# Five split weights and sixteen raw pages instead of seven and twelve in the SwiGLU blocks of a streaming-encoder layer

## The chip, the cores and the metric

The kernel runs on one core of a Trainium2 chip. The metric is the time of one execution on the device in microseconds (us), the median of the timed runs. The engines are TensorE (PE in the profile, PEld its weight loads), VectorE (DVE), ScalarE (ACT), GpSimd (POOL) and SyncE (SP). They run side by side, each through its own list of instructions in order, and wait for one another by semaphores. An instruction that waits holds up all that stands behind it on its engine.

## The reference

One layer on x of 256 rows by 2048 channels, in float32:

```python
x = _layer_norm(ALPHA * x + 0.5 * _swiglu(x, ffn1_w1, ffn1_w3, ffn1_w2), ln1_g, ln1_b)
mix = _hybrid_mixer(x, w_in, b_gates_m, conv_m, norm_m, w_up_m, w_up_sb, w_out)
x = _layer_norm(ALPHA * x + mix, ln2_g, ln2_b)
x = _layer_norm(ALPHA * x + 0.5 * _swiglu(x, ffn2_w1, ffn2_w3, ffn2_w2), ln3_g, ln3_b)
x = x + jax.nn.sigmoid(x @ w_ple_gate) * (p @ w_ple_proj)
```

where `_swiglu(x, w1, w3, w2)` is `(silu(x @ w1) * (x @ w3)) @ w2` with 5632 hidden channels. The mixer joins a chunkwise mLSTM and a stick-breaking attention. Only the two SwiGLU blocks, the first and the third line, have to do with the change.

## The kernel before

**Numbers.** Every float32 operand of a large matmul is split into a high part, rounded to the type that TensorE multiplies fast (fp32r), and a low part, the rest. A product is then three matmuls: high by high, high by low, low by high (L1061 to L1063). Activations stand transposed (`actT`) as the stationary operand, weights stream through.

**Pages.** One pool, `page_pool`, of 44 pages of 128 partitions by 1024 floats holds nearly everything: a raw weight as it was loaded (256 rows by 512 columns, one page), a split weight (two pages, high and low), the activations of 512 channels by 128 rows (one page) and the layer norms' vectors.

**Weights and units.** `program` is one long list. A `Unit` is one weight against 128 rows: two steps in depth of three matmuls, six in all. A plain weight serves two units, one for each half of the 256 rows. The last loop of the kernel (L1043) walks this list and writes each unit's matmuls; behind each unit it writes what has come due on the other engines.

**What a weight passes through.** SyncE loads it (L983, in `loads`). ScalarE writes the high part (L1010) and VectorE the low part (L1014), both in `split_one`. Then TensorE uses it. How far ahead this runs is set by `limits`: `splits_due` places the next split as long as fewer than `SPLIT_FFN` (7 before) split weights are held, counting the one in use. `loads` places the next load as long as fewer than `RAW_FFN` (12 before) raw pages are held and the pages suffice:

```python
while (pos["load"] < most and pos["raw"] < (4 if pos["at"] < 6 else limits(pos["split"])[0])
       and (mixing() or pages[0] + pos["raw"] + 2 * limits(pos["split"])[1] < PAGES - SPARE)):
```

`pages[0]` counts the activations' pages; `SPARE` was 1. In the mixer, and within six weights of the borders between the blocks (`EDGE`), other limits hold. They have names of their own (`RAW_MIX`, `SPLIT_MIX`, `RAW_EDGE`, `SPLIT_EDGE`).

**The SwiGLU blocks.** The hidden channels go in eleven chunks of 512. Three chunks (0, 5, 8) multiply x plainly with w1 and w3. The other eight use a scheme of seven products of half size in place of eight (`seven`, L314, in the manner of Strassen and Winograd), on both halves of the rows, with sums of weights and sums of activations. The sums of weights are made in the raw pages. Some are made by VectorE (L335). Others come by an accumulating transfer that GpSimd issues (L330): the first product's weight is split, then another quarter is added onto its raw page, then it is split again for the fifth product, added to again, split for the sixth, and once more, after a sum at L335, for the fourth. So the four quarter pages of a chunk stay taken from the first product to the fourth. A weight of these products serves one unit. `chained` (L355) strings the products of the eight chunks together, and `weave` (L157) mixes that chain about one to one with the main line: the plain products and those with w2. In the chain the sixth products follow the fifth by seven places.

**What comes due behind a unit.** A chunk's seven products end in three PSUM banks and two that stay (`seeded`). Copies and sums take them apart: L457 and L462 on ScalarE, L451 and L470 on VectorE. The hidden value, the silu of the gate times the up part, is made by VectorE at L473 for the first 128 rows and at L484 for the others. Eight planned microseconds later TensorE transposes it (L266, four matmuls against the identity), ScalarE writes the high part of the transpose (L268) and VectorE the low (L274). From then on the products with w2 may use it; each of them ends in an addition onto the residual (L497). The planner's time (`sched.now`) counts 0.2161 us for each matmul of 512 columns. All these instructions stand in the engines' lists between the splits, at the place where they came due. How many splits stand ahead of them is set by `SPLIT_FFN`.

Of the kernel before, what the change touches and what calls it, by code (L numbers as in the profile page):

```python
# [25 lines left out]
PAGES = 44  # L26
TEMP_BUFS = 6
FORMED = 8
SPARE = 1


RAW_FFN, RAW_MIX, RAW_EDGE = 12, 5, 4
SPLIT_FFN, SPLIT_MIX, SPLIT_EDGE = 7, 6, 11
EDGE = 6
PSUM_BUFS = 6
SKEW = 6
# [144 lines left out]
def kernel(  # L181
# [780 lines left out]
    def mixing():  # L962
        j = pos["split"]
        return any(-EDGE <= j - e < EDGE for e, _ in edges) or [m for e, m in edges if e <= j][-1:] == [True]

    def limits(j):

        if any(-EDGE <= j - e < EDGE for e, _ in edges):
            return RAW_EDGE, SPLIT_EDGE
        mixer = [m for e, m in edges if e <= j][-1:] == [True]  # L970
        return (RAW_MIX, SPLIT_MIX) if mixer else (RAW_FFN, SPLIT_FFN)
# [4 lines left out]
    def loads(most=len(raws)):  # L976
        while (pos["load"] < most and pos["raw"] < (4 if pos["at"] < 6 else limits(pos["split"])[0])
               and (mixing() or pages[0] + pos["raw"] + 2 * limits(pos["split"])[1] < PAGES - SPARE)):
            j = pos["load"]
# [121 lines left out]
```

## Time and profile before

| | us |
|---|---|
| median of 3 timed runs | 2291.09 (2286.04 to 2295.92) |
| profiled execution, its own time | 2298.76 |
| its span, first to last instruction | 2297.0 |
| first SwiGLU block, about | 30 to 700 |
| mixer, about | 700 to 1475 |
| second SwiGLU block, about | 1475 to 2160 |
| busy: TensorE, VectorE, ScalarE, GpSimd | 2228.0, 1681.4, 1231.7, 201.8 |

A row of the profile names the line of the kernel, the engine, the operation, and the tiles it writes and reads (`out<-in`, without buffer numbers), then how many there were. Rows of a timeline begin with start and length in us, and end, in brackets, with how long the engine was idle before and what ended it. Rows of waits name who waited and for whom, the us in total, how many times, and the longest. A stretch gives its ends and its length, then the busy us and the count of instructions for TensorE, its weight loads, VectorE, ScalarE and GpSimd, then the granted clock of TensorE, the busy share of the 16 DMA engines and the GB/s moved.

### The profile page before, as it was taken

Reading aid. Unit: us, or ns where it says so; the run is one execution under the profiler, and the core shown is the slowest. Engines: PE = TensorE matmul, PEld = TensorE weight load, DVE = VectorE, ACT = ScalarE, POOL = GpSimd, SP = SyncE. Lnnn points to the kernel's source line nnn. Section 1 sums busy time; section 2 is a strip of 40 time slices with the busy share of each in tenths; the row PEclk is TensorE's granted clock in tenths of the full one; section 3 lists DMA queues with packets and bytes.
Section 4 is the critical chain, followed back from the end, with each engine's and each line's share of the span. In section 5 each row is a group of like instructions: output and inputs, shape, how many; then the busy total and the mean of one; then the engine's idle time right before and its main releaser. Section 6 shows DMA issues by size and latency. Waiting matters only on the chain. (4 is left out here: it accounts for less than half of the span.)

```text
span 2297.0 us, 27486 instructions
## 1 busy us (share of the span) xinstructions
PE 2228.0 (97%) x10065; PEld 1835.2 (80%) x10065; DVE 1681.4 (73%) x1840; ACT 1231.7 (54%) x1441; POOL 201.8 (9%) x175
## 2 busy tenths in 40 slices
PE   9999989899999999999999999999998989999999
PEld 7878868778887888888888888787886877888878
DVE  6878877788898765654555466787886868889873
ACT  6656545555664555545653354465664555556552
POOL 3111001011100000100100000211011101100000
PEclk9999989999999999999999999999998999999999
DMA  9879869688894565665566666679886978979643
GB/s 322 232 214 298 223 186 285 198 257 231 265 307 164 180 187 162 175 185 145 177 183 188 188 227 219 183 197 273 250 216 187 296 189 245 300 229 295 230 153 100
DMA packets 262856, 501.83 MB, mean 218 GB/s; under 512 B 15744, under 2 KB 24768, under 8 KB 262720
## 3 DMA queue, kind: packets, MB, share of 16 engines
q1 hardware_dynamic: 227904, 432.95, 57.5%
q0 software_dynamic: 34816, 67.12, 16.5%
q8 instruction: 79, 1.29, 0.2%
q14 instruction: 57, 0.47, 0.1%
HBM read 497.91 MB, written 2.10 MB: 218 GB/s over the span
## 5 line engine op out<-in xcount | busy, mean ns | idle before, releaser
L1014 DVE TENSOR_TENSOR split<-raw,split 128x1024 fp32r<-128x1024 f32 (+1 forms) x1013 | 1180.7, 1203 | 328.3 <-ACT split L1010 318.9
L1010 ACT CAST split<-raw 128x1024 fp32r<-128x1024 f32 (+1 forms) x1013 | 1011.9, 1037 | 547.8 <-PE mm L1062 141.2
L1061 PE MATMUL mm<-split,actT 128*128 128x512 f32 (+2 forms) x2768 | 1084.9, 392 | 19.0 <-ACT actT L268 16.5
L1063 PE MATMUL mm<-split,actT 128*128 128x512 f32 (+2 forms) x2768 | 1074.6, 388 | 14.4 <-DVE actT L274 14.4
L1062 PE MATMUL mm<-split,actT 128*128 128x512 f32 (+2 forms) x2768 | 1071.8, 387 | 1.4 <-DVE split L1014 1.4
L1063 PEld LDWEIGHTS mm<-split,actT 128*128 128x128 f32 x2768 | 524.6, 190 | 126.7 <-DVE actT L274 21.6
L1061 PEld LDWEIGHTS mm<-split,actT 128*128 128x128 f32 x2768 | 525.0, 190 | 125.3 <-ACT actT L268 20.1
L1062 PEld LDWEIGHTS mm<-split,actT 128*128 128x128 f32 x2768 | 525.4, 190 | 103.9 <-DVE split L1014 2.6
L330 POOL DMA_DIRECT2D raw<-in_ffn_w_dram x128 | 156.0, 1230 | 1058.8 <-DVE split L1014 860.1
L335 DVE TENSOR_TENSOR raw<-raw 128x1024 f32<-128x1024 f32 x128 | 156.0, 1219 | 76.7 <-DMA raw<-in_ffn_w_dram 76.7
L1061 PE MATMUL seeded<-split,actT 128*128 128x512 f32 x384 | 151.6, 395 | 5.0 <-DVE seeded L451 5.0
L1062 PE MATMUL seeded<-split,actT 128*128 128x512 f32 x384 | 150.7, 392 | 0.8 <-DVE split L1014 0.8
L1063 PE MATMUL seeded<-split,actT 128*128 128x512 f32 x384 | 150.5, 392 | 0.0
L268 ACT CAST actT<-ms 128x512 fp32r<-128x512 f32 x84 | 49.1, 589 | 134.1 <-PE ms L266 116.9
L497 DVE SCALAR_TENSOR_TENSOR xres<-mm,xres 128x512 f32<-128x512 f32 x144 | 98.0, 683 | 10.3 <-PE mm L1063 10.1
L1061 PEld LDWEIGHTS seeded<-split,actT 128*128 128x128 f32 x384 | 72.8, 190 | 22.1 <-DVE seeded L451 7.1
L1062 PEld LDWEIGHTS seeded<-split,actT 128*128 128x128 f32 x384 | 72.8, 190 | 16.5 <-DVE split L1014 1.6
L1063 PEld LDWEIGHTS seeded<-split,actT 128*128 128x128 f32 x384 | 72.6, 189 | 15.3
L274 DVE TENSOR_TENSOR actT<-ms,actT 128x512 fp32r<-128x512 f32 x84 | 57.2, 685 | 30.8 <-ACT actT L268 19.7
L421 POOL TENSOR_SCALAR xres<-xres 128x512 f32<-128x512 f32 x16 | 28.2, 1877 | 319.7 <-DVE xres L404 300.5
L238 ACT ACTIVATE temp<-mm 128x512 f32<-128x512 f32 (+1 forms) x38 | 21.6, 573 | 52.6 <-PE mm L1063 52.6
L266 PE MATMUL ms<-ident,temp 128*128 128x128 f32 x176 | 28.9, 290 | 16.5 <-DVE temp L473 9.8
(124 smaller groups left out, 616.6 us busy)
## 6 DMA issues: line engine op xcount, KB each, us to landing
raw<-in_ffn_w_dram SPq DMA_DIRECT2D x527, 512.0 KB, 7.2
raw<-in_w_in_dram SPq DMA_DIRECT2D x168, 512.0 KB, 3.7
raw<-in_ffn_w_dram POOLq DMA_DIRECT2D x128, 512.0 KB, 9.6
raw<-in_w_out_dram SPq DMA_DIRECT2D x32, 512.0 KB, 4.8
raw<-in_w_ple_gate_dram SPq DMA_DIRECT2D x24, 512.0 KB, 5.0
raw<-in_w_up_m_dram SPq DMA_DIRECT2D x16, 512.0 KB, 3.7
raw<-in_w_up_sb_dram SPq DMA_DIRECT2D x16, 512.0 KB, 4.1
raw<-in_w_ple_gate_dram SPq DMA_DIRECT2D x16, 256.0 KB, 4.6
```

Of the source, the lines that this page charges most:

```text
L266: nc.tensor.transpose(ps[:, k], src[:, k * P:(k + 1) * P], ident[:])
L268: nc.scalar.copy(dst[:, 0], ps[:])
L274: nc.vector.tensor_tensor(out=dst[:, 1], in0=ps[:], in1=dst[:, 0], op=ALU.subtract)
L330: nc.gpsimd.dma_start(out=raw.tile[:, :, :cols], in_=src.src, accum_op=ALU.add)
L335: nc.vector.tensor_tensor(out=a.tile[:, :, :cols], in0=a.tile[:, :, :cols], in1=b.tile[:, :, :cols], op=ALU.add)
L421: nc.gpsimd.tensor_scalar(out=xs, in0=xs, scalar1=ALPHA, scalar2=None, op0=ALU.mult)
L497: nc.vector.scalar_tensor_tensor(out=xs, in0=ps, scalar=0.5, in1=xs, op0=ALU.mult, op1=ALU.add)
L1010: nc.scalar.copy(hi[:, ks], r[:, ks])
L1014: nc.vector.tensor_tensor(out=lo[:, ks], in0=r[:, ks], in1=hi[:, ks], op=ALU.subtract)
L1061: nc.tensor.matmul(ps, hi, w[0][:, k, :u.cols], start=first, stop=False, skip_group_check=u.onto)
L1062: nc.tensor.matmul(ps, hi, w[1][:, k, :u.cols], start=False, stop=False, skip_group_check=u.onto)
L1063: nc.tensor.matmul(ps, lo, w[0][:, k, :u.cols], start=False, stop=last, skip_group_check=u.onto)
```

## The change

Three numbers: in the SwiGLU blocks the splits that may be held fall from seven to five, the raw pages that may be held rise from twelve to sixteen, and the page limit leaves two pages free instead of one. Two split weights are four pages, which may now hold raw weights.

```diff
-SPARE = 1
+SPARE = 2
...
-RAW_FFN, RAW_MIX, RAW_EDGE = 12, 5, 4
-SPLIT_FFN, SPLIT_MIX, SPLIT_EDGE = 7, 6, 11
+RAW_FFN, RAW_MIX, RAW_EDGE = 16, 5, 4
+SPLIT_FFN, SPLIT_MIX, SPLIT_EDGE = 5, 6, 11
```

TensorE's list stays the same, and so does the number of instructions on every engine. What moves is where splits and loads stand against the rest. Two places show it.

VectorE, third chunk of the chain in the first block, from just behind the 24th sum at L335 to the product L473 (`xres` is the residual, `seeded` a PSUM bank that stays). Before:

```order
L1014 TENSOR_TENSOR split<-raw,split 128x1024
L497 SCALAR_TENSOR_TENSOR xres_86<-mm,xres_86 128x512
L1014 TENSOR_TENSOR split<-raw,split 128x1024
L497 SCALAR_TENSOR_TENSOR xres_87<-mm,xres_87 128x512
L1014 TENSOR_TENSOR split<-raw,split 128x1024 x5
L497 SCALAR_TENSOR_TENSOR xres_86<-mm,xres_86 128x512
L1014 TENSOR_TENSOR split<-raw,split 128x1024
L451 TENSOR_TENSOR temp<-seeded_79,temp 128x512
L1014 TENSOR_TENSOR split<-raw,split 128x1024
L497 SCALAR_TENSOR_TENSOR xres_87<-mm,xres_87 128x512
L1014 TENSOR_TENSOR split<-raw,split 128x1024
L473 SCALAR_TENSOR_TENSOR temp<-seeded_78,temp 128x512
```

The same place now, behind the same sum:

```order
L1014 TENSOR_TENSOR split<-raw,split 128x1024 x5
L497 SCALAR_TENSOR_TENSOR xres_86<-mm,xres_86 128x512
L1014 TENSOR_TENSOR split<-raw,split 128x1024
L451 TENSOR_TENSOR temp<-seeded_79,temp 128x512
L1014 TENSOR_TENSOR split<-raw,split 128x1024
L497 SCALAR_TENSOR_TENSOR xres_87<-mm,xres_87 128x512
L1014 TENSOR_TENSOR split<-raw,split 128x1024
L473 SCALAR_TENSOR_TENSOR temp<-seeded_78,temp 128x512
```

Ten splits stood between the sum and L473, and now eight do; two residual additions that came behind the sum now come ahead of it.

ScalarE, first chunk of the chain in the first block, around the copy L268 of a transposed hidden value. The numbers tell pages apart. Before, raw_797, raw_821, raw_894 and raw_908 are the four quarter pages of the next chunk, here split for its sixth products:

```order
L238 ACTIVATE temp_1041<-temp_1041 128x512
L1010 CAST split_1302<-raw_797 128x1024
L1010 CAST split_1312<-raw_821 128x1024
L1010 CAST split_1322<-raw_894 128x1024
L457 COPY temp_1339<-mm_1281 128x512
L268 CAST actT_1347<-ms_1342 128x512
L1010 CAST split_1351<-raw_1149 128x1024
L1010 CAST split_1364<-raw_908 128x1024
```

Now the four quarter pages are raw_592, raw_695, raw_869 and raw_889:

```order
L238 ACTIVATE temp_1036<-temp_1036 128x512
L1010 CAST split_1296<-raw_1097 128x1024
L1010 CAST split_1308<-raw_1111 128x1024
L1010 CAST split_1320<-raw_592 128x1024
L457 COPY temp_1337<-mm_1276 128x512
L268 CAST actT_1345<-ms_1340 128x512
L1010 CAST split_1349<-raw_695 128x1024
L1010 CAST split_1360<-raw_869 128x1024
```

Three of the quarter pages were split ahead of the copy, and now one is; the second and third follow it.

## The prediction

> **What bounds the kernel now.** I read the engine totals first, to see whether anything is left to gain, then the stretches table, to find where, then the waits of TensorE inside the two SwiGLU blocks, to see for whom it waits.
>
> ```profile
> span 2297.0 us, 27486 instructions
> PE 2228.0 (97%) x10065; PEld 1835.2 (80%) x10065; DVE 1681.4 (73%) x1840; ACT 1231.7 (54%) x1441; POOL 201.8 (9%) x175
> ```
>
> TensorE is busy 97% of the span, so a change that moves no matmul can only fill its holes. Where they are shows in the stretches. Columns: length, busy time and count of each engine, granted clock, share of the DMA engines, GB/s. The first row is a stretch without a hole, the next two are the blocks, the last six are the stretches with the worst holes.
>
> ```profile
> 60.00:120.00 60.00, 60.00 (x270) 49.68 (x269) 50.73 (x48) 38.26 (x43) 8.41 (x7) 1.00 0.89 236
> 30.00:700.00 670.00, 643.60 (x2808) 526.74 (x2808) 551.54 (x545) 392.81 (x424) 78.84 (x65) 0.98 0.87 250
> 1475.00:2160.00 685.00, 662.60 (x2913) 542.80 (x2912) 571.66 (x565) 402.39 (x435) 85.61 (x69) 0.98 0.85 244
> 120.00:180.00 60.00, 55.32 (x229) 44.54 (x228) 46.02 (x48) 31.84 (x34) 4.87 (x4) 0.91 0.76 217
> 300.00:360.00 60.00, 52.50 (x212) 42.33 (x213) 45.43 (x46) 28.69 (x31) 5.88 (x5) 0.89 0.68 182
> 360.00:420.00 60.00, 54.02 (x227) 43.33 (x226) 42.23 (x39) 32.13 (x37) 6.20 (x6) 0.94 0.80 223
> 1560.00:1620.00 60.00, 55.15 (x238) 44.35 (x237) 48.22 (x50) 32.15 (x35) 7.28 (x6) 0.97 0.83 227
> 1740.00:1800.00 60.00, 50.59 (x206) 40.28 (x205) 46.20 (x48) 30.16 (x32) 6.08 (x5) 0.89 0.63 174
> 1800.00:1870.00 70.00, 64.11 (x272) 51.55 (x271) 51.12 (x48) 37.41 (x41) 8.46 (x7) 0.95 0.82 228
> ```
>
> A hole costs twice: the idle time, and the matmuls after it that run at half clock. Idle time of the six stretches (length less PE busy): 4.7 + 7.5 + 6.0 + 4.9 + 9.4 + 5.9 = 38.4 us. Half clock (one less the granted clock, times the length): 5.4 + 6.6 + 3.6 + 1.8 + 6.6 + 3.5 = 27.5 us. Together **66 us**. Both blocks whole have 26.4 + 22.4 = 48.8 us idle and 0.02 × 1355 = 27 us of clock, 76 us, so the six stretches hold most of it. Whom does TensorE wait for there? In the first block (us in total, times, longest):
>
> ```profile
> PE mm L1061 <- ACT actT L268: 8.1, 5, 3.4
> PE ms L266 <- DVE temp L473: 4.3, 1, 4.3
> PE ms L266 <- DVE temp L484: 2.8, 1, 2.8
> PE mm L1062 <- DVE split L1014: 0.6, 1, 0.6
> PE seeded L1062 <- DVE split L1014: 0.4, 1, 0.4
> ```
>
> The second block:
>
> ```profile
> PE mm L1061 <- ACT actT L268: 8.4, 5, 3.5
> PE ms L266 <- DVE temp L473: 5.5, 1, 5.5
> PE ms L266 <- DVE temp L484: 2.6, 1, 2.6
> ```
>
> It hardly ever waits for a split (1.0 us in the first block). It waits for the hidden values: the product of gate and up part (L473, L484 on VectorE) and the copies after its transpose (L268 on ScalarE). These are short operations that stand in line behind splits for weights that TensorE needs much later. The timeline of VectorE before the wait of 4.3 us:
>
> ```profile
> 280.43 1.23 DVE L335 TENSOR_TENSOR raw<-raw 128x1024 f32<-128x1024 f32 x1 [2.84 <-DMA raw<-in_ffn_w_dram]
> 287.06 1.23 DVE L335 TENSOR_TENSOR raw<-raw 128x1024 f32<-128x1024 f32 x1 [1.93 <-DMA raw<-in_ffn_w_dram]
> 291.68 5.83 DVE L1014 TENSOR_TENSOR split<-raw,split 128x1024 fp32r<-128x1024 f32 x5
> 302.62 0.68 DVE L473 SCALAR_TENSOR_TENSOR temp<-seeded,temp 128x512 f32<-128x512 f32 x1
> ```
>
> VectorE loses 2.84 + 1.93 = 4.8 us because raw weights for the sum at L335 land late, then it works without a pause from 287.06 to 303, ten splits among it, and comes to L473 about 4 us late. The other kind of hole comes from ScalarE:
>
> ```profile
> 148.00 1.05 ACT L1010 CAST split<-raw 128x1024 fp32r<-128x1024 f32 x1 [2.94 <-DMA raw<-in_ffn_w_dram]
> 151.95 1.04 ACT L1010 CAST split<-raw 128x1024 fp32r<-128x1024 f32 x1 [2.90 <-DMA raw<-in_ffn_w_dram]
> 153.38 0.59 ACT L268 CAST actT<-ms 128x512 fp32r<-128x512 f32 x1
> 154.02 0.50 PE L1061 MATMUL mm<-split,actT 128*128 128x512 f32 x1 [2.66 <-ACT actT L268]
> ```
>
> Two splits wait, at the head of ScalarE's line, for accumulating transfers into their raw pages; the copy L268 stands behind both, and TensorE for the copy.
>
> **Part by part.** *1. Two splits fewer ahead of each short operation.* No instruction is added or removed, and TensorE's order is the same. 131 of the 151 VectorE operations of the first block that are neither splits nor L335 sums move ahead by two splits, the other 20 by none. In the first place VectorE does eight splits, not ten, between the sum of 287.06 and L473. In the second, L268 comes ahead of the two waiting splits. Prices of a split:
>
> ```profile
> L1014 DVE TENSOR_TENSOR split<-raw,split 128x1024 fp32r<-128x1024 f32 (+1 forms) x1013 | 1180.7, 1203 | 328.3 <-ACT split L1010 318.9
> L1010 ACT CAST split<-raw 128x1024 fp32r<-128x1024 f32 (+1 forms) x1013 | 1011.9, 1037 | 547.8 <-PE mm L1062 141.2
> ```
>
> Where VectorE is behind, each short operation comes 2 × 1.2 = 2.4 us earlier. By this alone L473 has 4.3 − 2.4 = 1.9 and 5.5 − 2.4 = 3.1 us left, L484 0.4 and 0.2 us: 5.6 us. The waits for L268 go, because 2.94 + 2.90 us of waiting moves behind the copy, more than its longest wait of 3.5 us. After a rest of 3.1 us I count one more run at half clock, 3.4 us, the half of a stretch of about 7 us as the row of 1800 to 1870 has it: 9.0 us remain of the 66.
>
> *The clock.* In the row at 154.02 a wait of 2.66 us is enough for the half clock that the stretch 120 to 180 shows (0.91). The Trainium skill, "TensorE: Matmul & The Clock Gate", Part 1, has it that the clock falls after an idle window of about 3.4 us and comes back after as long a busy one; by that the rest of 3.1 us would cost only itself, and 5.6 us would remain instead of 9.0. The trace's 2.66 us (with 1.35 us two matmuls later) speaks for the smaller bound, so the sum keeps 9.0.
>
> *2. Raw pages earlier.* A load is placed only while activation pages, raw pages and twice the allowed splits stay under the limit. Activation and raw pages together can reach 32 (42 less 10) and not 29 (43 less 14); the cap of 16 is met only where activations are few. Three pages matter most where raw pages are pinned: from the first product of a chunk to its fourth, its four quarter pages are not given back. The worst such place (two stretches, then VectorE's wait):
>
> ```profile
> 565.00:578.00 13.00, 11.57 (x54) 9.16 (x54) 11.59 (x13) 8.88 (x11) 0.00 (x0) 1.00 0.00 1
> 600.00:610.00 10.00, 10.00 (x45) 8.28 (x45) 1.86 (x3) 2.59 (x3) 0.00 (x0) 1.00 1.09 297
> 609.69 1.22 DVE L335 TENSOR_TENSOR raw<-raw 128x1024 f32<-128x1024 f32 x1 [8.14 <-DMA raw<-in_ffn_w_dram]
> ```
>
> For 13 us nothing is moved at all (share 0.00), since SyncE's queue stands at a load whose page is not free; 25 us later the transfers cannot keep up (1.09) and VectorE starves for 8.1 us. In the program two loads at this place move ahead by 12 and 13 splits. Counted over the first block, a load's place is a median of five TensorE units (part 3: 1.33 us each) further ahead of its split's place, 6.6 us. What a load takes to land:
>
> ```profile
> raw<-in_ffn_w_dram SPq DMA_DIRECT2D x527, 512.0 KB, 7.2
> raw<-in_ffn_w_dram POOLq DMA_DIRECT2D x128, 512.0 KB, 9.6
> L335 DVE TENSOR_TENSOR raw<-raw 128x1024 f32<-128x1024 f32 x128 | 156.0, 1219 | 76.7 <-DMA raw<-in_ffn_w_dram 76.7
> ```
>
> VectorE's waits for raw pages at L335 are 76.7 us in 26 times, nearly all below 3 us, so 6.6 us more would hide them, if the DMA engines have the room: 0.87 and 0.85 of them are busy over the blocks, and a block shorter by 30 us raises that to 0.91. The gain that this adds on TensorE is at most the 9.0 us that remain plus the 10 us of small holes (76 − 66); I take none of it, and let it only keep part 3 small.
>
> *3. Less split work in hand.* The next split is placed while fewer than seven (now five) are held, the one in use included. So six, now four, lie ahead; weights that serve two units alternate with weights that serve one, so that is 9 units and now 6. A unit is six matmuls, and 270 in 60 us make 0.222 us each, 1.33 us a unit: 12 us in hand, now 8. A split costs 1.0 on ScalarE and 1.2 on VectorE one after the other, which leaves 9.8 and now 5.8 us. But the starvation of 8.1 us at 609.69 let TensorE wait 1.0 us, so the real reserve was 7.1; less 4.0 it is 3.1. Bounds: nothing, if the 8.1 us goes with part 2; and if it stays, 5 us idle and 3.4 us of half clock in each block, 17 us. No gain below nothing: a split that is placed later cannot be early. I take half, **8 us**, as the transfers' room is good but not proved.
>
> *4. The rest.* SyncE places two more loads ahead of the norms' vectors at the end of each block, some 75 us before these are used. On GpSimd the second block's first accumulation goes behind three more scalings:
>
> ```profile
> L421 POOL TENSOR_SCALAR xres<-xres 128x512 f32<-128x512 f32 x16 | 28.2, 1877 | 319.7 <-DVE xres L404 300.5
> ```
>
> 3 × 1.88 = 5.6 us; its page is split again some 14 units later (three more of the chain, ten or eleven of the main line), 14 × 1.33 = 19 us, which covers 5.6 + 9.6 = 15.2. Without that cover it would cost 5.6 us once. The mixer and the tail keep their limits.
>
> **Sum.** 66 − 9 − 8 = 49 us off the profiled execution: 2298.8 (span 2297.0 and 1.8 around it) becomes 2249.8. It lies 0.33% above the median of the three timed runs, 2291.1; the same 49 us off the median give **2242 us**.
>
> **The rivals.**
> - *Raw pages land no earlier* (the DMA engines are the limit in the stretches that matter). For: 1.09 at 600 to 610. Against: 0.00 just before it, idle that only the page limit explains. Then part 3 costs 17 us, and pairs of waits of 4.8 us reach past the reserve of 3.1 by 1.7 us some five times in each block: 17 + 17 = 34 instead of 8. 66 − 9 − 34 = 23 off: 2268.
> - *Slower: the splits become what TensorE waits for.* Place: the 26 sums at L335 in the two blocks. If VectorE is usually so far behind that the shorter reserve is zero, every wait for a raw page reaches TensorE: 77 us, and some 12 us of half clock after the longest. 66 − 9 − 89 = −32: 2323. It decides from the point where more than 57 of the 89 us get through, a reserve below about 1 us. For: VectorE is busy 82% of the blocks, and its work comes in bursts. Against: the reserve of 7.1 us measured at the worst place.
> - *The change doesn't do what it says*: the page limit, not the cap, decides, and activations eat the three pages. The short operations still move, but new holes of the same size open at other places of the chain, as VectorE has the same work. About 2291, from 2280 to 2302. For: all 16 chunks have the same chain, and only some now show holes, so chance has a part. Against: the order puts the two waiting splits behind the copy in every chunk alike.
>
> **How the numbers follow.** Forecast 0.66 (own range 2222 to 2262, from 69 us off, when half of the small holes go too and part 3 costs nothing, to 29 off); raw pages no earlier 0.14 (2262 to 2280); the same 0.10; slower 0.10. A measurement of this kernel tells about 0.5%, 11.5 us, from no change. Faster: 0.66 + 0.14 = 0.80; within: 0.10; slower: 0.10. The range reaches from 2222 up through the second case and half of the third, to 2290; left out are the slower case, the other half of the third and a little of the forecast's ends, 0.18.
>
> **What would show it.** Right: in the stretches that answer to the six, PE busy near its length and a clock of 1.00; no wait for L473, L484 and L268 above 2 us; DVE waits at L335 for a raw page well below 76.7 us; no DMA share near 0.00 within a block. Part 3 too small: waits of TensorE for L1014 above 8 us in sum. The forecast is wrong if the waits for L473 and L268 stay, or if waits for L1014 take their place.

## The result, and the profile after

The kernel after the change takes 2253.55 us (median of 4 runs, 2250.64 to 2255.85). The kernel before, run beside it, takes 2291.83 us (4 runs, 2286.04 to 2295.92). The ratio is 0.9834, 95% interval 0.9809 to 0.9859: 1.7% faster. The profiled execution took 2255.85 us, 42.9 us less than that of before, where the forecast took off 49.

The totals of the page of after:

```profile
span 2254.1 us, 27470 instructions
PE 2213.1 (98%) x10065; PEld 1828.4 (81%) x10065; DVE 1682.6 (75%) x1840; ACT 1237.8 (55%) x1441; POOL 201.9 (9%) x175
```

The other engines do the same work (the 16 instructions fewer in the count are waits for semaphores); TensorE, with the same matmuls, is busy 14.9 us less. That is less time at half clock: the granted clock over the span is 0.993, where it was 0.985. The trace places the gain: the mixer's first step on TensorE (L550) starts at 682.1 us instead of 704.7, its last norm step (L407) at 1448.8 instead of 1470.4, the last norm step of the second block at 2161.1 instead of 2203.9. So the first block gave 22.6 us, the mixer lost 1.0, and the second block gave 21.2.

The stretches of after. First the two blocks whole, then the stretches that answer to the six bad ones (they lie earlier now, by up to 40 us):

```profile
30.00:685.00 655.00, 639.90 (x2822) 526.12 (x2822) 554.89 (x548) 393.74 (x421) 78.75 (x66) 0.99 0.89 261
1448.00:2117.00 669.00, 659.66 (x2932) 543.36 (x2931) 572.58 (x566) 408.58 (x440) 81.91 (x67) 0.99 0.87 250
120.00:180.00 60.00, 58.14 (x260) 47.57 (x259) 53.03 (x54) 34.69 (x37) 6.01 (x5) 1.00 0.86 243
290.00:350.00 60.00, 55.37 (x237) 44.55 (x236) 47.00 (x48) 31.83 (x36) 7.01 (x6) 0.97 0.76 202
360.00:420.00 60.00, 56.95 (x241) 46.19 (x240) 44.98 (x43) 34.74 (x38) 4.85 (x4) 0.94 0.76 222
1560.00:1620.00 60.00, 58.32 (x254) 47.55 (x253) 50.57 (x53) 34.83 (x39) 7.22 (x6) 0.97 0.81 227
1700.00:1760.00 60.00, 55.38 (x237) 44.51 (x237) 48.90 (x51) 32.62 (x34) 6.04 (x5) 0.97 0.79 221
1800.00:1860.00 60.00, 58.18 (x260) 47.67 (x259) 47.81 (x46) 36.57 (x40) 8.01 (x8) 1.00 0.80 221
```

Idle time of the six: 1.9 + 4.6 + 3.0 + 1.7 + 4.6 + 1.8 = 17.6 us; half clock 1.8 + 3.6 + 1.8 + 1.8 = 9.0 us. **27 us** are left of the 66, and the forecast left 9. The blocks whole have 15.1 + 9.3 = 24.4 us idle and 0.01 × 1324 = 13 us of clock, 38 of 76 us (the clock is rounded to hundredths, so this is good to some 7 us).

Whom TensorE waits for now, in the first block:

```profile
PE mm L1061 <- ACT actT L268: 5.5, 4, 2.9
PE ms L550 <- DMA temp<-in_conv_m_dram: 3.1, 1, 3.1
PE mm L1063 <- DVE actT L274: 2.5, 3, 1.7
PE ms L266 <- DVE temp L484: 1.8, 1, 1.8
PE ms L266 <- DVE temp L473: 1.5, 1, 1.5
PE mm L1062 <- DVE split L1014: 0.8, 1, 0.8
```

and in the second:

```profile
PE mm L1061 <- ACT actT L268: 3.3, 4, 1.2
PE ms L266 <- DVE temp L484: 1.7, 1, 1.7
PE mm L1063 <- DVE actT L274: 1.6, 2, 0.9
PE ms L266 <- DVE temp L473: 1.5, 1, 1.5
PE mm L1062 <- DVE split L1014: 1.2, 1, 1.2
```

Of the kernel before, these rows belong beside them, two of the first block and two of the second, which the prediction's lists leave out:

```profile
PE mm L1063 <- DVE actT L274: 4.5, 3, 1.7
PE seeded L1061 <- DVE seeded L451: 3.0, 3, 1.1
PE mm L1063 <- DVE actT L274: 2.6, 2, 1.3
PE seeded L1061 <- DVE seeded L451: 2.0, 2, 1.1
```

The longest wait for a hidden value falls from 5.5 to 2.9 us, and splits did not take the place of these waits. With both blocks added up, the idle time went from 48.8 to 24.4 us, mostly like this: L268 16.5 to 8.8, L473 9.8 to 3.0, L484 5.3 to 3.5, L274 7.1 to 4.1. L451 (5.0) and the residual's additions L497 (3.5) have no row any more: these are short operations behind splits too. Raw pages come in time: the sum at L335 waits 11.5 us in all, where it was 76.7, though a load takes longer to land (median 8.4 us, was 7.2).

```profile
L335 DVE TENSOR_TENSOR raw<-raw 128x1024 f32<-128x1024 f32 x128 | 155.7, 1217 | 11.5 <-DMA raw<-in_ffn_w_dram 11.5
```

Two of the waits that stayed show why. VectorE before L484 in the third chunk of the chain:

```profile
292.04 1.21 DVE L1014 TENSOR_TENSOR split<-raw,split 128x1024 fp32r<-128x1024 f32 x1
293.17 0.68 DVE L473 SCALAR_TENSOR_TENSOR temp<-seeded,temp 128x512 f32<-128x512 f32 x1
293.77 1.21 DVE L1014 TENSOR_TENSOR split<-raw,split 128x1024 fp32r<-128x1024 f32 x1
295.22 0.69 DVE L274 TENSOR_TENSOR actT<-ms,actT 128x512 fp32r<-128x512 f32 x1 [0.23 <-ACT actT L268]
299.70 1.23 DVE L1014 TENSOR_TENSOR split<-raw,split 128x1024 fp32r<-128x1024 f32 x1 [3.79 <-PE mm L1062]
300.85 0.68 DVE L484 SCALAR_TENSOR_TENSOR temp<-seeded,temp 128x512 f32<-128x512 f32 x1
```

VectorE is not behind here: it stands idle for 3.79 us. But the split at the head of its line waits for a matmul (L1062, the one that reads low halves), so for a page which TensorE has still to give back, and L484 starts as soon as that split is through. It was the same before the change, in the same chunk (ScalarE's row, then VectorE's):

```profile
309.55 1.04 ACT L1010 CAST split<-raw 128x1024 fp32r<-128x1024 f32 x1 [4.44 <-PE mm L1062]
310.63 1.22 DVE L1014 TENSOR_TENSOR split<-raw,split 128x1024 fp32r<-128x1024 f32 x1 [4.79 <-ACT split L1010]
311.77 0.68 DVE L484 SCALAR_TENSOR_TENSOR temp<-seeded,temp 128x512 f32<-128x512 f32 x1
```

There ScalarE's half of the split waited for the page, and VectorE's half for ScalarE's. Now only VectorE's half waits, and TensorE's wait for L484 is shorter by 1.0 us (2.77 and 1.75 us), the length of ScalarE's half. ScalarE before L268 in the fourth chunk:

```profile
392.77 1.04 ACT L1010 CAST split<-raw 128x1024 fp32r<-128x1024 f32 x1 [2.40 <-DMA raw<-in_ffn_w_dram]
393.72 0.58 ACT L268 CAST actT<-ms 128x512 fp32r<-128x512 f32 x1
```

Here one split still stands ahead of the copy and waits for its accumulating transfer. TensorE's wait of 2.9 us is this one.

### The profile page after: what moved, and what is told of

Read it like the earlier page. It is cut to its first block, busy times and chain, and to the rows that moved or that the text cites. A ratio compares the mean times of both kernels' runs of the same rounds, so it can differ in the third digit from the quotient of the medians.

```text
span 2254.1 us, 27470 instructions
## 1 busy us (share of the span) xinstructions
PE 2213.1 (98%) x10065; PEld 1828.4 (81%) x10065; DVE 1682.6 (75%) x1840; ACT 1237.8 (55%) x1441; POOL 201.9 (9%) x175
## 5 line engine op out<-in xcount | busy, mean ns | idle before, releaser
L1014 DVE TENSOR_TENSOR split<-raw,split 128x1024 fp32r<-128x1024 f32 (+1 forms) x1013 | 1183.0, 1203 | 331.7 <-ACT split L1010 298.0
L1062 PE MATMUL mm<-split,actT 128*128 128x512 f32 (+2 forms) x2768 | 1069.1, 386 | 2.6 <-DVE split L1014 2.6
L1062 PEld LDWEIGHTS mm<-split,actT 128*128 128x128 f32 x2768 | 523.3, 189 | 104.0 <-DVE split L1014 3.7
L335 DVE TENSOR_TENSOR raw<-raw 128x1024 f32<-128x1024 f32 x128 | 155.7, 1217 | 11.5 <-DMA raw<-in_ffn_w_dram 11.5
L1062 PE MATMUL seeded<-split,actT 128*128 128x512 f32 x384 | 150.0, 391 | 0.0
L268 ACT CAST actT<-ms 128x512 fp32r<-128x512 f32 x84 | 49.1, 589 | 131.4 <-PE ms L266 131.2
L497 DVE SCALAR_TENSOR_TENSOR xres<-mm,xres 128x512 f32<-128x512 f32 x144 | 97.9, 683 | 21.4 <-PE mm L1063 21.4
L1063 PEld LDWEIGHTS seeded<-split,actT 128*128 128x128 f32 x384 | 72.4, 188 | 15.1
L1062 PEld LDWEIGHTS seeded<-split,actT 128*128 128x128 f32 x384 | 72.4, 189 | 15.1
L274 DVE TENSOR_TENSOR actT<-ms,actT 128x512 fp32r<-128x512 f32 x84 | 57.1, 684 | 30.1 <-ACT actT L268 18.9
L238 ACT ACTIVATE big<-mm 128x512 f32<-128x512 f32 x20 | 12.0, 598 | 55.8 <-PE mm L1063 55.8
```

Source lines behind the costliest of these rows:

```text
L238: nc.scalar.activation(out, in_, func, **kw)
L268: nc.scalar.copy(dst[:, 0], ps[:])
L274: nc.vector.tensor_tensor(out=dst[:, 1], in0=ps[:], in1=dst[:, 0], op=ALU.subtract)
L335: nc.vector.tensor_tensor(out=a.tile[:, :, :cols], in0=a.tile[:, :, :cols], in1=b.tile[:, :, :cols], op=ALU.add)
L497: nc.vector.scalar_tensor_tensor(out=xs, in0=ps, scalar=0.5, in1=xs, op0=ALU.mult, op1=ALU.add)
L1014: nc.vector.tensor_tensor(out=lo[:, ks], in0=r[:, ks], in1=hi[:, ks], op=ALU.subtract)
```

## The experiments

**Theory.** The gain comes from order: urgent short operations stand behind fewer splits in the lines of VectorE and ScalarE. **Rivals.** The raw pages carry the gain, or a part of it, since transfers start earlier. Or the reserve of splits was already on the edge, and a further cut of it loses at once. What is called the limit below is the number that activation and raw pages may reach together: 29 before the change, 32 after it.

### The order of the splits without the raw pages

`split5_old_raw` is the kernel after with the limit put back to 29 and the cap of raw pages to 12, so that, against the kernel before, limit and cap are the same and only the number of splits differs:

```diff
-SPARE = 2
-RAW_FFN, RAW_MIX, RAW_EDGE = 16, 5, 4
+SPARE = 5
+RAW_FFN, RAW_MIX, RAW_EDGE = 12, 5, 4
```

> Five splits, but the raw pages as before the change: with five splits reserved, a page limit of 39 lets activation and raw pages together reach 29, as before, and the cap is twelve again. Both parts matter (theory): the short operations come two splits earlier, but the sums at L335 still wait for raw pages (between 40 and 80 us), and with the smaller reserve part of that reaches TensorE: about 2270 us, 2260 to 2282. Order alone (rival): as the changed kernel, 2254. Raw pages alone (rival): as before or slower, 2290 or more.

Measured: 2253.44 us (2251.86 to 2257.35), ratio to before 0.9836 (0.9813 to 0.986). This is the whole gain of the change, as far as the intervals can tell, so the time that was expected of order alone (there the rival) is the one that came, and the theory that both parts matter does not hold for the time. The waits of TensorE:

```profile
PE mm L1062 <- DVE split L1014: 7.3, 7, 3.1
PE mm L1061 <- ACT actT L268: 7.0, 8, 2.1
PE ms L266 <- DVE temp L473: 7.0, 2, 3.5
```

The rival that raw pages carry the gain falls. That they did nothing would be wrong too: with 29 the waits for splits are 7.7 us and with 32 they are 2.6 over the span, L473 7.0 and 3.1. But with 32 there is L484 (3.5 us; with 29 it has no row), L268 is 8.8 instead of 7.0, and the step L550 at the border waits 3.1 us for a transfer, with 29 only 0.3. Gain and loss cancel. The sum at L335 waits 38.6 us here, so more than half of its fall from 76.7 to 11.5 came without a page: under the same limit a split that is placed later leaves its load further ahead of it. What this does for VectorE is in the gain of 38 us as well, and no run takes it apart from the order.

### How many splits

Three kernels change `SPLIT_FFN` in the kernel after, with `SPARE` set so that the limit stays near 32. `split6_raw31` has 6 and 1 (a limit of 31), `split4_new_raw` 4 and 4, `split3_new_raw` 3 and 6 (both 32). Six splits with 32 pages (`split6_new_raw`, `SPARE` 0, 44 pages in all) have no time: that program deadlocks. Seven splits with 32 pages would need 46 pages, so raw pages alone, with the old order, could not be tried. The edit for four:

```diff
-SPARE = 2
+SPARE = 4
...
-SPLIT_FFN, SPLIT_MIX, SPLIT_EDGE = 5, 6, 11
+SPLIT_FFN, SPLIT_MIX, SPLIT_EDGE = 4, 6, 11
```

> Six splits, cap sixteen, activation and raw pages together up to 31 (spare 1). After the run with five splits and the old raw pages, the order of splits and short operations is the theory for the whole gain, and raw pages the rival. Order: six splits stand halfway, each short operation comes one split earlier than before, about 2272 us, 2262 to 2282, with waits for L473, L484 and L268 between the two kernels' (before 29 us in the two blocks, changed kernel 15). Raw pages: two of the three pages are there, 2255 to 2262.

Measured: 2263.36 us (2262.61 to 2264.12), ratio 0.9877 (0.9862 to 0.9893). L268 is 12.9 us, L484 5.5, L473 3.1. The time lies at the edge of both expectations, so it does not decide between them.

> Four splits, raw pages as in the changed kernel (spare 4). Theory: the short operations come one more split earlier and the holes at L473, L484 and L268 shrink further, but the reserve of splits, measured at 4.2 us in the median with five, falls to about 2 us, so waits of TensorE for L1014 rise from 3 us to 10 to 25 us: 2258 us, 2246 to 2272. Order alone: 12 to 19 us better than five, about 2238. Raw pages alone: no change, 2254.

Measured: 2247.59 us (2244.55 to 2252.11), ratio 0.981 (0.9784 to 0.9835). Its interval overlaps that of the change, so four is not shown to be better than five. The waits for L1014 are 4.6 us, and the expected rise to 10 to 25 did not come.

> Three splits, raw pages as in the changed kernel (spare 6). Theory: two weights are in hand, about 4 us of matmuls, of which a split takes 2.3 us; every burst of short operations on VectorE reaches TensorE, and waits for L1014 and L1010 are above 50 us: slower than the changed kernel, 2290 to 2340. Order alone: better again, below 2235. Raw pages alone: no change, 2254.

Measured: 2269.46 us (2267.79 to 2274.21), ratio 0.9911 (0.9882 to 0.9939), faster than expected. Of its waits for splits the matmuls of TensorE show 7.0 us and the weight loads this:

```profile
PEld mm L1062 <- DVE split L1014: 26.1, 49, 1.7
```

Seven, six, five, four and three splits give about 2292, 2263, 2254, 2248 and 2269 us. By the medians each split fewer gains down to four, by less each time; the step from seven to six also brings two pages. At three, two lie ahead of the one in use, and the loss comes as many short waits for splits: by the weight loads 26.1 us in 49 waits, none above 1.7, where four splits have 4.4 us in three; the time rises by 21.9. So the edge lies at three, and the rival that the change already stood on it falls. With four splits, and with three alike, the waits for L268 and L473 are 8 of 0.7 us and 2 of 1.5 us, 8.5 us in all. For L268 that is the length of the chain itself, as the copy starts when the transposes end (294.60 and 294.57 us in the kernel after) and TensorE has nothing else in its list. At L473, where six, five, four and three splits all give 1.5 us with 31 or 32 pages, one split still stands directly ahead: in the kernel after, the last matmul before the wait ends at 292.38, the split begun at 292.04 is still at work, and L473 starts behind it at 293.17. So holding fewer splits does not shorten this wait. Whether another order would was not tried.

### Taking the hurry away

The six places lie at the chunks of the chain whose products with w2 stand right behind the chunk's end in TensorE's list. If that is why the short operations are urgent, giving TensorE other work there must remove these holes at any number of splits. In the line below, `down(c)` are the products of chunk c with w2, `gate` and `hidden` those of the plain chunks 0, 5 and 8. The edit moves plain products ahead of `down(1)` and `down(3)`, and `down(5)` ahead of `down(4)`:

```diff
-        main = flat(hidden[0] + gate[1] + down(0) + down(1) + hidden[1] + down(2) + down(3) + gate[2] + down(4, 5) + hidden[2] + down(6)
+        main = flat(hidden[0] + gate[1] + down(0) + hidden[1] + down(1) + down(2) + gate[2] + down(3) + down(5, 4) + hidden[2] + down(6)
```

`before_late_use` is the kernel before with this line, `after_late_use` the kernel after, `split4_late_use` the one with four splits. Nothing is left out; only the residual's additions come in another order.

> The kernel before, with only the main line of both blocks in another order: the products of the hidden chunks 1, 3 and 4 with w2 stand 16, 16 and 4 units later behind the chunk's end. Theory (a hole opens only where a product with w2 stands so close behind the end of its chunk that every short operation must be prompt): four of the six holes go and two shrink, although VectorE and ScalarE are as late as before: 2250 us, 2235 to 2268. Rival (lateness by itself makes the hole, wherever the use is): the holes at L473, L484 and L268 stay or move, 2282 to 2300.

Measured: 2255.7 us (2250.42 to 2258.32), ratio 0.9841 (0.9821 to 0.9861): as much as the change, without it. The waits for L473, L484 and L268 have no row any more. Behind seven splits as ever, these short operations keep TensorE waiting in the blocks:

```profile
PE seeded L1061 <- DVE seeded L451: 13.7, 7, 6.0
PE mm L1061 <- DVE xres L497: 3.5, 3, 1.5
```

L451 was 5.0 us with no wait above 1.1, so a part of the lateness did move, as the rival has it, to the next short operation that TensorE needs soon.

> The changed kernel with the same reordered main line. Theory: what is left of the holes at L473, L484 and L268 (15 us and their half clock) goes for the most part: 2232 us, 2222 to 2242. Rival (lateness by itself): no change, 2248 to 2258, or worse, as three more pages of hidden values are held and the raw pages shrink by as much.

Measured: 2223.84 us (2223.47 to 2225.33), ratio 0.9706 (0.9691 to 0.9721): faster than both kernels by intervals that don't touch theirs. Its blocks:

```profile
30.00:656.00 626.00, 623.80 (x2789) 516.43 (x2790) 545.92 (x539) 392.13 (x421) 77.32 (x64) 1.00 0.92 266
1390.00:2066.00 676.00, 672.53 (x3017) 556.01 (x3016) 583.28 (x592) 408.67 (x445) 91.42 (x72) 1.00 0.88 256
```

2.2 + 3.5 = 5.7 us idle are left, and a clock of 1.00. Fewer splits and later use nearly add up: 38 and 35 us alone, 67 together. They close the same holes at L473, L484 and L268, but L451 and L497, the short operations that later use leaves urgent, have no row with five splits.

> Four splits (spare 4) with the reordered main line. Theory: both means close the same holes, so little is added to the reordered kernel with five splits: 2230 us, 2220 to 2242. If they were independent, the 6 us by which four splits were better than five would add to the reordering's gain in full. Rival: as four splits alone, 2248.

Measured: 2228.81 us (2225.91 to 2230.29), ratio 0.9726 (0.9706 to 0.9746): not better than five, and by the medians 5.0 us worse, though the intervals overlap. With the later use, going from five splits to four brings nothing more.

### What the raw pages are worth

`split5_raw27` is `split5_old_raw` with `SPARE = 7`, a limit of 27. `split5_old_late` is `split5_old_raw` with the later use (29). The kernels with 29 pages and fewer also have the old cap of 12.

> Five splits in the order of use of the change, with raw and activation pages together limited to 27 (29 before the change, 32 after it). Going from 29 to 32 moved nothing in time though the waits for raw pages at L335 fell from 38.6 to 11.5 us. Theory A, raw pages are worth nothing over the whole span 27 to 32: 2253 us within 6, with L335 waits of 50 to 70 us. Theory B, the reserve of splits only just covers the waits at 29: TensorE waits for L1014 rise from 7.7 to 20 us or more, and the time to 2265 to 2280 us.

Measured: 2261.94 us (2260.9 to 2264.81), ratio 0.9872 (0.9844 to 0.99). L335 waits 53.9 us, TensorE 11.3 + 2.6 = 13.9 us for splits, less than theory B had, and the time comes out between the two.

> Five splits, raw and activation pages together limited to 29 as before the change (not 32), and the later use of the chunks in the main line. With the old order of use, the three more raw pages were worth nothing, because a gain on the waits for splits (7.7 to 2.6 us) was given back at L484 and at the border. Theory A, the raw pages are worth nothing here: as with 32 pages and later use, 2224 us within 5. Theory B, with the holes behind the hidden values gone nothing is given back, so the raw pages show their own worth: TensorE waits some 7 us for splits at L1014 instead of 1.9, with one or two runs at half clock of 3.4 us: 2230 to 2236 us.

Measured: 2229.47 us (2227.81 to 2230.14), ratio 0.9731 (0.9708 to 0.9754). The waits for splits are 8.5 + 0.3 us, those at L335 37.5. The time lies above the range of theory A, by 0.5 us, and below that of theory B, by as much. Since this ran on another chip than its partner, the pair was run once more on one chip, with a limit of 28 (`SPARE = 6`) beside it:

> The change (five splits, raw and activation pages together limited to 32) with the later use of the chunks, once more, on the same chip as the same kernel with limits of 29 and 28. On different chips 32 gave 2223.84 and 29 gave 2229.47 us, with intervals that touch. Theory B, raw pages have a worth of their own once the holes behind the hidden values are gone: 2224 us, at least 4 below the kernel with 29. Theory A, they are worth nothing: within 2 us of it.

> Five splits, the later use, limit of 29. Theory B: 2229 us, at least 4 above the kernel with 32. Theory A: within 2 us of it.

> Five splits, the later use, limit of 28. Theory B: a page fewer costs more near the edge, as from 29 to 27 in the order of the change (8.5 us): 2231 to 2237 us, with waits for splits at L1014 of 10 us or more. Theory A: within 2 us of the kernel with 32.

Measured: with 32 2224.59 us (2222.88 to 2225.84), ratio 0.9716 (0.9703 to 0.9729); with 29 2229.8 us (2226.94 to 2230.06), 0.9734 (0.972 to 0.9747); with 28 2239.64 us (2235.85 to 2241.89), 0.978 (0.9767 to 0.9794). Between 32 and 29 no run of one lies among those of the other, and the medians are 5.2 us apart here and 5.6 on the two chips; the intervals still overlap by a tenth of a per cent. Theory B holds, and one page below 29 costs more than expected. The sum at L335 waits 12.0, 36.8 and 51.2 us in the three. TensorE waits 2.2, 8.9 and 15.7 us for L1014 in them. So with the holes gone the three pages of the change are worth some 5 us, and the page below them some 10. With 28 the longest wait for a raw page is as long as the longest of before, and it can be followed to TensorE (VectorE's row, then TensorE's):

```profile
577.97 1.23 DVE L335 TENSOR_TENSOR raw<-raw 128x1024 f32<-128x1024 f32 x1 [8.12 <-DMA raw<-in_ffn_w_dram]
580.38 0.50 PE L1062 MATMUL mm<-split,actT 128*128 128x512 f32 x1 [3.40 <-DVE split L1014]
```

Of 8.12 us 3.40 reach TensorE: the reserve of five splits is 4.7 us at this place.

### All medians

| splits held | limit | order of before, us | later use, us |
|---|---|---|---|
| 7 | 29 | 2291.8 | 2255.7 |
| 6 | 31 | 2263.4 | |
| 5 | 32 | 2253.6 | 2223.8 and 2224.6 |
| 5 | 29 | 2253.4 | 2229.5 and 2229.8 |
| 5 | 28 | | 2239.6 |
| 5 | 27 | 2261.9 | |
| 4 | 32 | 2247.6 | 2228.8 |
| 3 | 32 | 2269.5 | |

Beside them, in the order of before, TensorE's waits for the short operations and for splits (L1014), and VectorE's at the sum L335, in us over the span:

| splits held | limit | L268 | L473 | L484 | L1014 | L335 |
|---|---|---|---|---|---|---|
| 7 | 29 | 16.5 | 9.8 | 5.3 | 2.2 | 76.7 |
| 6 | 31 | 12.9 | 3.1 | 5.5 | 0.6 | 10.8 |
| 5 | 32 | 8.8 | 3.1 | 3.5 | 2.6 | 11.5 |
| 5 | 29 | 7.0 | 7.0 | no row | 7.7 | 38.6 |
| 5 | 27 | 5.5 | 7.7 | no row | 13.9 | 53.9 |
| 4 | 32 | 5.4 | 3.1 | no row | 4.6 | 11.7 |
| 3 | 32 | 5.4 | 3.1 | no row | 7.0 | 8.5 |

L268 falls as fewer splits are held, and more pages do not lower it. L473 goes mostly with the pages: it is at 3.1 us wherever there are 31 or 32. With five splits and 29 pages VectorE loses 3.98 us to a late raw page at a sum L335, some 12 us ahead of the first L473 that is late, and works without a pause from there to it.

## Why the prediction was right

The forecast of 2242 us, range 2222 to 2290, has the measured 2253.55 inside its likeliest case (2222 to 2262). The mechanism was right in the main, and two terms of the sum had the wrong size, on opposite sides; that they cancel in part is luck.

**Holes behind short operations: right.** They are the gain. It stays whole when the raw pages are taken back (2253.44), grows by the medians with each split fewer down to four, and comes in equal size when the urgency is removed instead (2255.7). It is plainest at L268. Its share at L473 was overrated: two splits fewer alone took 9.8 us to 7.0 there, not to 5.0, and the other 3.9 us came from the raw pages, from which the sum took nothing. That 3.0 us are left in the blocks, near the forecast 5.0, is luck.

**"9.0 us remain of the 66": too small, 27 remain.** By parts, idle time in the two blocks: L473 was to keep 1.9 + 3.1 = 5.0 and kept 3.0; L484 was to keep 0.6 and kept 3.5; L268 was to go and kept 8.8; L274, which is not in the prediction's lists, kept 2.4 in the six stretches (5.4 before); half clock was to take 3.4 more and took 9.0 there. For L268 the step said that "the waits go, because 2.94 + 2.90 us of waiting moves behind the copy". That removed what the splits put on top, but not the floor of 8 × 0.7 = 5.4 us that four splits leave as well: the copy itself, for which TensorE has no other work. The other 3.4 us are nearly all at three of the eight copies, where one split still stands ahead and waits for its accumulating transfer, 2.40 us in the row above (1.23 and 1.18 us by the trace of the other two). At L484 the step that failed is a reading: the sum took 2.4 us off each wait because VectorE would be less behind, but in the kernel before it was not behind there. It stood idle for 4.79 us, since the split ahead of L484 waited for a page, and it still does, for 3.79 us. That wait is there with seven and six splits too, and has no row with four, or with five and a limit of 29; why was not followed. A shorter line helps as far as the wait is work in the line; where it is an instruction that itself waits, that instruction has to move behind the short operation, as it did at L268.

**"Less split work in hand costs 8": too large.** TensorE waits 2.0 us for splits in the blocks. Two steps failed in the same direction. The reserve was put at 7.1 − 4.0 = 3.1 us, and 4.7 us are measured. And the bound took the wait of 8.1 us as staying in part; with 32 pages the longest waits at that place are these:

```profile
590.15 1.23 DVE L335 TENSOR_TENSOR raw<-raw 128x1024 f32<-128x1024 f32 x1 [3.38 <-DMA raw<-in_ffn_w_dram]
596.69 1.22 DVE L335 TENSOR_TENSOR raw<-raw 128x1024 f32<-128x1024 f32 x1 [1.91 <-DMA raw<-in_ffn_w_dram]
599.11 0.50 PE L1062 MATMUL mm<-split,actT 128*128 128x512 f32 x1 [0.77 <-DVE split L1014]
```

Of 3.38 + 1.91 = 5.3 us 0.8 reach TensorE, a reserve of about 4.5. What lies outside the six stretches, splits with it, is about 38 − 27 = 11 us where the forecast left 10 + 8 = 18. In sum 38 us remain and not 27, so the forecast was 11 us too low by the stretches (good to some 7), by the medians (38.3 us off and not 49) 11, and by the two profiled executions (42.9 off) 6. The low end of the range does not follow from its own terms either: with half of the small holes gone too and nothing lost to splits they give 66 − 9 + 5 = 62 us off, 2229 us, and not 69 off.

**Raw pages, taken at nothing: right as a sum, by luck.** In the order of the change 32 pages and 29 are 0.1 us apart. Under it lie a gain at L1014 and L473 and a loss at L484, L268 and L550, which happen to cancel. With later use the same three pages are worth some 5 us. The prediction read the waits at L335 as nearly all below 3 us: 18 of the 26 are, and the other eight hold 37 of the 76.7 us. Its conclusion stands all the same, since only two of them are above 6.6. The Trainium skill, "Perfetto Trace Analysis", Optimization Strategy, has it that consistent bubbles on the engine that should be saturated can mean too little memory for the next tile. In this case that is the smaller part: 38 us came with five splits and no page more, 5 us with the pages, and these showed only with the later use.

**Signs that failed.** One wait for L268 is still above 2 us (2.89), and the clock is 1.00 in two of the six stretches only. "No DMA share near 0.00 within a block" fails as well. The place that answers to 565 to 578:

```profile
545.00:558.00 13.00, 13.00 (x63) 10.78 (x62) 12.43 (x15) 8.16 (x10) 0.00 (x0) 1.00 0.09 14
```

SyncE's queue still stands at a load whose page is not free, with a share of 0.09. It costs little, since the pages that are already loaded last longer: TensorE is busy all 13 us, and the wait of 8.14 us that followed is 3.38.

**The rivals.** Raw pages no earlier: no, 76.7 became 11.5 us. Splits become the bound: no, 2.0 us in the blocks, and even three splits stay faster than before by 0.9%. Holes of the same size elsewhere: no; the holes that are left stand at the same places of the chain.

**What stays open.** Why the border step L550 waits 2.8 to 5.7 us for its vectors in some of these kernels and hardly at all in others (0.3 us with five splits and 29 pages, 0.4 or no row with the later use added to these) was not followed. Nor was it followed why L268 is longer with 32 pages than with 29.

## What to carry to other kernels

On an engine that works through its list in order, work placed far ahead of need stands in front of work that is needed now. So the depth of a prefetch has a price in every short urgent operation behind it, and it should be as deep as its reserve needs and no deeper (here four or five, where seven cost 38 us). Before the depth is tuned, ask why the short operation is urgent: giving the bounding engine other work for that moment removed the holes at L268, L473 and L484 with seven splits and with five, floor and all; with seven a part came back at the next short operation, and the two together gave 67 us. Look, too, whether the engine in the way is at work or idle: a short operation can stand behind one instruction that waits, and then a shorter line alone need not help. Here the extra buffers showed their worth only when the holes beside them were gone.

## What the runs showed of the hardware

Short idle times were enough for half clock. TensorE in the kernel after, around the waits for L473 and L268 (rows left out lie 0.42 us apart before 298.4, then closer):

```profile
291.99 0.39 PE L1063 MATMUL seeded<-split,actT 128*128 128x512 f32 x1
293.91 0.66 PE L266 MATMUL ms<-ident,temp 128*128 128x128 f32 x4 [1.53 <-DVE temp L473]
295.24 0.80 PE L1061 MATMUL mm<-split,actT 128*128 128x512 f32 x1 [0.68 <-ACT actT L268]
...
297.54 0.63 PE L1063 MATMUL mm<-split,actT 128*128 128x512 f32 x1
297.96 0.63 PE L1061 MATMUL mm<-split,actT 128*128 128x512 f32 x1
...
299.00 0.39 PE L1061 MATMUL mm<-split,actT 128*128 128x512 f32 x1
299.22 0.39 PE L1062 MATMUL mm<-split,actT 128*128 128x512 f32 x1
```

After 1.53 and 0.68 us of idle with four small matmuls between, the matmuls start about 0.42 us apart instead of 0.22, from 295.24 to 298.76, 3.5 us. After the wait of 2.89 us at 394.35 the slow run lasts to 401.29 by the same timeline, 6.9 us, twice that. At the second pair of waits, 1.75 and 0.67 us at 301.59 and 302.92, the starts were slow for about 1 us only. So the length of the idle time alone does not tell the price. The Trainium skill, "TensorE: Matmul & The Clock Gate", Part 1, has a fall after an idle window of about 3.4 us, and a window that runs freely. The runs of 3.5 and 6.9 us agree with the window's length; that an idle time must fill a window is not what these rows show. The prediction took the 2.66 us of its trace as enough for half clock, and less was enough: the 9.0 us of half clock left in the six stretches follow waits of 0.7 to 2.9 us.

The DMA engines had the room that the prediction left open. With later use and 32 pages they move the first block's bytes in 626 us, where the kernel before took 670: a share of 0.92 at 266 GB/s instead of 0.87 at 250, and the sum at L335 waits 10.8 us over the span instead of 76.7.
